# A hybrid backbone block (GDN, RWKV-7, mLSTM, mixture of experts): paired RWKV inverses, mLSTM on another chain, dense products in groups of six

## The chip, the cores and the metric

The kernel runs on one core of a Trainium2 chip. The metric is the device time of one execution in microseconds (us), the median of several runs. The profile is of one execution; its times count from the first instruction.

## The reference

Four layers. A layer takes 256 context tokens and 256 latent tokens of 1024 channels, modulates their RMS norm, and projects them by one matrix into the inputs of three mixers, each run in both directions, and 3 x 1024 gate columns. The three results are projected, gated, summed and projected again; a mixture of 16 experts follows. In the last layer the context tokens only feed states, and nothing else of them is computed.

```python
for l in range(DEPTH):
    gdn_x, rwkv_x, mlstm_x, gate_x = split_cols(modulate(rmsnorm(x)) @ w_in[l], col_groups)
    ...                                    # the same for the context tokens
    a_c, a_x = gdn_branch(...)             # 4 heads of 128: a unit lower triangular solve per chunk of 64, a scan
    b_c, b_x = rwkv_branch(...)            # 8 heads of 64: S_t = S_{t-1}(diag(w_t) + a_t b_t^T) + v_t k_t^T
    m_c, m_x = mlstm_branch(...)           # 4 heads, keys of 64, values of 128, stabilised by a running max
    x = x + mod_x[2] * (sum(sigmoid(gates[i]) * (branches[i] @ w_branch[i]) for i in range(3)) @ w_out[l])
    x = x + mod_x[5] * moe_ec(...)         # expert choice: each expert takes its best 32 tokens of 256
```

Latent scans start from the last state of the context scan of the same direction.

## The kernel before

All activations lie transposed, 128 channels by 512 tokens (256 of context, 256 latent). A layer's **scan stage** holds the input projection and the three mixers; behind it come the gated sum of the branches, the output projection and the experts.

**Dense products.** A block of 128 output columns is `w_in` (line 461): `load_w` brings the weights in two tiles of four 128x128 blocks, ScalarE rounds each to a high part (line 363), GpSimd subtracts to a low part (line 364), and `dense` (378) sums for each of eight k the products high x high, high x low and low x high, 24 products of 128x512 (256 wide in the last layer) into one PSUM bank. Two banks take such blocks: "dm" those that a mixer reads (31 a layer), "df" 36 fillers (gate columns, mLSTM's inputs), whose results go to DRAM.

**Order.** The program is not ordered by hand. Each instruction gets a priority from a planned time ("due", `at`, line 239), smaller first, and a list scheduler puts on each engine the ready instruction with the smallest one; the order is fixed when the program is built. `Stream.due` and `spend` move a mixer's due time on as its products are issued, by its pace. Before, RWKV has 240 due units per pair of heads (`D_R`), GDN 170 per head (`D_G`), mLSTM begins at 680 with pace 12 (`P_M`), and the fillers are spread over 1000. In `dense` three k (`CH`) share one due time, and anything with an earlier one may step in between two products. `go_on` (245) gives what follows the first call everywhere; only `ada`, the modulation's products, uses it.

**RWKV** runs four pairs of heads one after another on the PSUM banks "ai" and "ac". A pair has two units, context (`st` 0) and latent (`st` 1). A unit: `rwkv_prep` (decays, keys and so on, mostly VectorE, line 786), the masked products M (893), the transposes, `tri_inverse`, and four chunk steps (926). `rwkv_prep` of the next unit is issued inside `tri_inverse` of this one (`between`).

**`tri_inverse`** (393) inverts 16 systems of 64x64. They go to DRAM and come back as their 64 diagonal blocks of 16x16, a block per partition (so on 64 of 128 partitions); 14 column steps of two VectorE instructions invert these (413, 414); they go to DRAM and come back in place, and four rounds of 16 small products (437 to 440) give the inverse. GDN uses it once a head.

**GDN** runs four heads one after another on the banks "bi" (eight chunk steps a head, line 1120), and **mLSTM** follows GDN on the same banks, beside RWKV's last pairs. The first branch that is gated and projected, within mLSTM's stage, is GDN's; RWKV's and mLSTM's follow together behind the scans.

Of the kernel before, what the change touches and what calls it, by code (L numbers as in the profile page):

```python
# [12 lines left out]
U32 = mybir.dt.uint32  # L13
# [67 lines left out]
CH = 3  # L81
DT = BLK / 8 * 1.0
D_R, D_G = 240.0, 170.0
P_R, P_G, P_M = D_R * 2.6 / 240, D_G * 3.5 / 170, 12.0
# [68 lines left out]
def tile_backbone(ctx: ExitStack, tc: tile.TileContext, A, out, dbg=None, depth=DEPTH):  # L153
# [32 lines left out]
    for pi in ("ai", "bi"):  # L186
        systems[pi] = (dp.tile([2, 8, 4160], F32, tag="zi" + pi, bufs=1, name="zi" + pi),
                       dp.tile([2, 2, 8, 4160], F32, tag="zo" + pi, bufs=1, name="zo" + pi))
# [70 lines left out]
    with tc.tile_pool(name="zero", bufs=1) as p0:  # L259
        zero = p0.tile([128, 1040], F32, name="zero")  # L260
        gp.memset(zero, 0.0)
        for _, zo in systems.values():
            sy.dma_start(zo.rearrange("w p q x -> (w p q x)").rearrange("(a b) -> a b", a=128), zero)
# [30 lines left out]
    def ada(l, P, g, pool=None, bufs=2, t=None):  # L294
# [98 lines left out]
    def tri_inverse(z, src, sys, between=None):  # L393
        zi, zo = z.dram
        for p in range(2):
            sy.dma_start(zi[p, :, 0:4096].rearrange("q (r c) -> r q c", c=64), src(p))

        def blocks(t):
            return t.rearrange("p q x -> (p q x)").rearrange("(m x) -> m x", x=1040)[:, 0:1024].rearrange("m (r c) -> m r c", c=64)[:, :, 0:16]
        bt, sol = z.mt([2, 16, 16], "Y"), z.mt([2, 16, 16], "Z")  # L400
        bt, Xb = bt[0:64, 0], bt[0:64, 1]
        tr = "m r c -> m c r"
        sy.dma_start(bt, blocks(zi))
        md = [C[f"dir{d}"][0:64].bitcast(U32)[:, :, None].to_broadcast([64, 16, 16]) for d in range(2)]
# [10 lines left out]
        TU = z.mt([2, 8, 64], "TU")  # L415
        for w in range(2):
            xw, xo = (Xb, Xb.rearrange(tr)) if w == 0 else (Xb.rearrange(tr), Xb)
            se.copy(sol[0:64, w], xw)
            ve.copy_predicated(sol[0:64, w], md[1], xo)
            sy.dma_start(blocks(zo[w]), sol[0:64, w])  # L420
            for p in range(2):
                sy.dma_start(TU[64 * p:64 * p + 64, w], zo[w, p, :, 0:4096].rearrange("q (r c) -> r q c", c=64))
        T, U = TU[:, 0], TU[:, 1]
# [12 lines left out]
        Z, Y = z.mt([8, 64], "Z"), z.mt([8, 64], "Y")  # L436
        ve.tensor_tensor(Z, pz, C["off"][:, None, :].to_broadcast([128, 8, 64]), ALU.mult)
        last = U
        for _ in range(3):
            ve.tensor_tensor(Y, products(lambda p, hp, q: Z[hp, q, :], lambda p, hp, q: last[hp, q, :]), U, ALU.add)  # L440
            last = Y
        return T, U, Y
# [13 lines left out]
    def layer(l, P, last, ahead):  # L456
# [14 lines left out]
        gates = dp.tile([36, 128, 512], F32, tag="gates", name=nm("gates"))  # L471
# [9 lines left out]
        def first_branch():  # L481
# [3 lines left out]
            for b in range(4):  # L485
                t = w2k("lom")
                sy.dma_start(t[:, n], spill[0][:, b, n])
                split(ab[:, 0, b, n], ab[:, 1, b, n], t[:, n], gp)
            for db in range(8):
                at(AM0 + AMS * db)  # L490
                th = w2k("rawm")
                gated(0, db, (ab[:, 0], ab[:, 1]), th, "f")
                sy.dma_start(part[db][:, n], th[:, n])

        def second_branch():
            ab = big(F32R, (2, 4, 512))
            for b in range(4):
                t = wp.tile([128, 512], F32, tag=("him", "lom")[b % 2], bufs=2, name=nm("mg"))
                sy.dma_start(t[:, n], spill[1][:, b, n])
# [3 lines left out]
        def other_branches(z, rwkv_):  # L503
# [3 lines left out]
            for db in range(8):  # L507
                t1, th = t2(), t2() if db else wp.tile([128, 512], F32, tag="rawm", bufs=2, name=nm("mg"))
                gated(2, db, mlstm_, th, "f")
                gated(1, db, rwkv_, t1, "m")  # L510
# [9 lines left out]
        with scope("rwkv", "ai", "ac", 3) as zr:  # L520

            xT = X["sb"]
            r = rms_scale(zr, X["ss"], 0, "sgd")
            if l > 0:
                X["dram"] = dp.tile([128, 8, 512], F32, tag="xd", name=nm("xd"))
                sy.dma_start(X["dram"], xT)
            hh, hl = big(F32R), big(F32R)
            for k in range(8):
                t = zr.mt([512], "t2")
                ve.tensor_tensor(t, xT[:, k, :], r, ALU.mult)  # L530
                for s in range(2):
                    ts_ = t[:, s * 256:(s + 1) * 256]
                    ve.tensor_scalar(ts_, ts_, der[:, 0, k, s:s + 1], mod[:, k, s:s + 1], ALU.mult, ALU.add)
                split(hh[:, k, :], hl[:, k, :], t, gp)

            clock["base"] = tc.cur_priority + 100000


            todo = [(B_GATE + i, i) for i in range(24)] + [(B_MO + i, 24 + i) for i in range(4)]
            todo[FM:FM] = [(b + i, 28 + q + i) for b, q, m in ((B_MK, 0, 2), (B_MQ, 2, 2), (B_MV, 4, 4)) for i in range(m)]  # L540
            for t, (b, i) in zip(FILL, todo):
                c0 = 0 if i in (28, 29, 32, 33, 34, 35) else oc
                ps = w_in(b, t, c0, "f")
                th = common.mt([512], "gt", 1)
                if i < 28:
                    se.activation(th[:, c0:], ps[:, c0:], AF.Tanh, scale=0.5)  # L546
                else:
                    se.activation(th[:, c0:], ps[:, c0:], AF.Copy, scale=0.125 if i in (30, 31) else 1.0)
                sy.dma_start(gates[i][:, c0:], th[:, c0:])
            ahead()  # L550

            at(0)
            with scope("pre", "bi", "bi", 3) as z:
                G = small_gates(z, l, P, hh, hl)
            R = rwkv_begin(zr, l, P, w_in, oc)
            pair = [rwkv_inputs(zr, l, 0, P, R, w_in, oc)]
            S = {}

            def rwkv(b):
                rwkv_pair(zr, l, b, P, R, pair, S, spill[1], last, oc)  # L560
            with scope("gdn", "bi", "bi", 3) as zg:
                head = [gdn_inputs(zg, l, 0, P, w_in, oc), gdn_inputs(zg, l, 1, P, w_in, oc)]

                def gdn(h):
                    gdn_head(zg, l, h, P, head[h], G, spill[0], oc, D_G * h)
                pair.append(rwkv_inputs(zr, l, 1, P, R, w_in, oc))
                rwkv(0)
                gdn(0)
                head.append(gdn_inputs(zg, l, 2, P, w_in, oc))
                gdn(1)  # L570
                pair.append(rwkv_inputs(zr, l, 2, P, R, w_in, oc))
                rwkv(1)
                head.append(gdn_inputs(zg, l, 3, P, w_in, oc))
                gdn(2)
                pair.append(rwkv_inputs(zr, l, 3, P, R, w_in, oc))
                gdn(3)
            with scope("mlstm", "bi", "bi", 3) as zm:
                rwkv(2)
                rwkv(3)
                mlstm(zm, l, P, G, gates, oc, D_G * 4, first_branch)  # L580
                at(1500)
                rwkv_ = second_branch()


        with scope("moe", "ai", "bi") as z:
            W = Weights(z, l)
            rt = route_begin(z, l, P, last)
            mh, ml = other_branches(z, rwkv_)
# [1132 lines left out]
```

## Time and profile before

| | |
|---|---|
| median of 3 runs | 5148.35 us (5140.02 to 5159.23) |
| profiled execution | 5153.63 us, span 5151.7 us |
| busy: PE, VectorE, ScalarE, GpSimd | 4671.7, 3135.1, 1437.8, 1401.7 us |
| granted TensorE clock, mean | 0.95 |

PE is TensorE's products, PEld its weight loads, DVE VectorE, ACT ScalarE, POOL GpSimd, SPq the queue that issues all DMAs. The ends of products are modelled, so rows of PE overlap: the time that a product costs is read from start to start. Layer 1's scan stage runs from about 1420 to 2270 us, layer 3's from 4010 to 4790.

### The profile page before, as it was taken

The page shows a single profiled execution, that of the slowest core. Times are in us where ns is not written, and L with a number is a line of the kernel's source. Part 1 is how long each engine was busy: PE and PEld are TensorE (multiplying, and loading weights), DVE is VectorE, ACT ScalarE, POOL GpSimd, SP SyncE. Part 2 cuts the span into 40 slices and gives each one's busy share as a digit, 9 for nine tenths or more (in the row PEclk, how much of TensorE's full clock was granted, in tenths as well). Part 3 has the DMA queues.
Part 4 walks back from the last instruction along what each step waited for, and adds up shares of the span by engine and source line. Part 5 has one row for each costly group of instructions (what it writes and reads, how often), then busy time and mean ns, then how long its engine had stood idle before and what let it go on. Part 6 is the DMA issues. An engine that isn't in the chain of part 4 may idle for free. (4 is left out here: it accounts for less than half of the span.)

```text
span 5151.7 us, 85291 instructions
## 1 busy us (share of the span) xinstructions
PE 4671.7 (91%) x31882; PEld 2965.9 (58%) x31882; DVE 3135.1 (61%) x8787; ACT 1437.8 (28%) x2796; POOL 1401.7 (27%) x1847
## 2 busy tenths in 40 slices
PE   7999999999999989999998999999998898888698
PEld 4666666653466666665336666666633666666533
DVE  4777766633477876663347778666333688767322
ACT  3333232320233322222023323232201433222211
POOL 3333212320243332232014322223301433323400
PEclk8999999999999999999999999999999899987899
DMA  5334345679632233457972223345696222223598
GB/s 189 110 101 119 121 137 172 205 272 393 246 90 80 81 98 121 137 167 264 394 273 92 84 70 105 100 137 164 234 392 260 86 70 72 81 66 115 185 385 316
DMA packets 677006, 873.59 MB, mean 170 GB/s; under 512 B 336976, under 2 KB 359504, under 8 KB 663792
## 3 DMA queue, kind: packets, MB, share of 16 engines
q1 hardware_dynamic: 676592, 868.14, 50.0%
q8 instruction: 251, 4.11, 0.3%
q14 instruction: 163, 1.34, 0.1%
HBM read 788.47 MB, written 79.51 MB: 168 GB/s over the span
## 5 line engine op out<-in xcount | busy, mean ns | idle before, releaser
L364 POOL TENSOR_TENSOR wlo<-wraw,whi 128x512 fp32r<-128x512 f32 x696 | 938.3, 1353 | 2198.2 <-ACT whi L363 1649.3
L386 PE MATMUL df<-big,whi 128*128 128x512 f32 (+1 forms) x2944 | 1001.9, 408 | 87.6 <-ACT gt L546 19.7
L386 PE MATMUL dm<-big,whi 128*128 128x512 f32 (+1 forms) x2368 | 821.2, 415 | 44.6 <-ACT cv L693 31.7
L363 ACT CAST whi<-wraw 128x512 fp32r<-128x512 f32 x696 | 426.3, 617 | 1159.1 <-PE df L386 481.8
L386 PEld LDWEIGHTS df<-big,whi 128*128 128x128 f32 x2944 | 545.8, 200 | 253.9 <-issue 46.9
L386 PE MATMUL df<-big,wlo 128*128 128x512 f32 (+1 forms) x1536 | 612.0, 398 | 16.6 <-POOL wlo L364 16.6
L386 PEld LDWEIGHTS dm<-big,whi 128*128 128x128 f32 x2368 | 443.0, 199 | 174.6 <-issue 40.5
L386 PE MATMUL dm<-big,wlo 128*128 128x512 f32 (+1 forms) x1248 | 505.6, 405 | 18.3 <-POOL wlo L364 18.3
L386 PEld LDWEIGHTS df<-big,wlo 128*128 128x128 f32 x1536 | 306.3, 199 | 83.8 <-POOL wlo L364 20.9
L1607 PE MATMUL df<-mw,big 128*64 128x512 f32 x1024 | 301.3, 610 | 0.0
L386 PEld LDWEIGHTS dm<-big,wlo 128*128 128x128 f32 x1248 | 248.1, 199 | 81.2 <-POOL wlo L364 22.7
L1654 DVE SCALAR_TENSOR_TENSOR big<-bi,der,big 128x256 f32<-128x256 f32 x448 | 191.9, 478 | 118.4 <-PE bi L1651 117.9
L1607 PE MATMUL dm<-mw,big 128*64 128x512 f32 x1024 | 255.6, 594 | 2.3 <-DMA mw<-in_w_dram 2.3
L997 DVE SCALAR_TENSOR_TENSOR cv<-cv,par,cv 128x189 f32<-128x189 f32 (+3 forms) x472 | 231.3, 499 | 18.3 <-ACT cv L994 14.3
L1614 POOL MEMSET mada<- 128x512 f32 x32 | 16.8, 525 | 800.6 <-PE bi L1651 351.1
L414 DVE TENSOR_TENSOR Y<-Y,sv 64x14 f32<-64x14 f32 (+6 forms) x672 | 193.6, 290 | 5.6
L413 DVE TENSOR_TENSOR sv<-Y 64x14 f32<-64x14 f32 (+6 forms) x672 | 183.2, 275 | 5.4
L1607 PEld LDWEIGHTS dm<-mw,big 128*64 128x64 f32 x1024 | 80.7, 137 | 152.5 <-issue 137.8
L1645 DVE SCALAR_TENSOR_TENSOR mlof<-ac,aff,mhif 128x512 fp32r<-128x512 f32 x32 | 24.0, 750 | 212.4 <-ACT mhif L1644 212.4
L697 DVE SCALAR_TENSOR_TENSOR big<-cv,muc,big 128x252 f32<-128x252 f32 (+2 forms) x280 | 140.4, 515 | 21.0 <-ACT big L694 19.4
L1641 PE MATMUL ac<-mw,mrawf 128*64 128x512 f32 x512 | 139.6, 600 | 8.6 <-ACT mrawf L1635 8.5
L210 PE MATMUL ai<-AR,BK 64*128 64x128 f32 (+1 forms) x1024 | 133.4, 308 | 10.4 <-DVE M L893 6.1
(511 smaller groups left out, 7965.2 us busy)
## 6 DMA issues: line engine op xcount, KB each, us to landing
mw<-in_w_dram SPq DMA_DIRECT2D x768, 512.0 KB, 10.3
wraw<-in_w_in_dram SPq DMA_DIRECT2D x536, 256.0 KB, 2.7
adaw<-in_ada_w_dram SPq DMA_DIRECT2D x96, 1024.0 KB, 6.2
gates<-gt SPq DMA_DIRECT2D x114, 256.0 KB, 2.9
wraw<-in_w_branch_dram SPq DMA_DIRECT2D x96, 256.0 KB, 2.9
TU<-zoai SPq DMA_DIRECT2D x128, 128.0 KB, 3.1
wraw<-in_w_out_dram SPq DMA_DIRECT2D x64, 256.0 KB, 6.7
t<-gates SPq DMA_DIRECT2D x61, 256.0 KB, 4.1
```

Of the source, the lines that this page charges most:

```text
L210: mm(o, a, b, **kw)
L363: se.copy(dst_hi, src)
L364: eng.tensor_tensor(dst_lo, src, dst_hi.bitcast(F32), ALU.subtract)
L386: mm(ps[:, c0:c1], a[:, k % 4, :], bk[:, c0:c1], start=(n == 0), stop=(n == 3 * nk - 1))
L413: ve.tensor_tensor(tv, Xb[:, j + 1:, j:j + 1].to_broadcast(sh), Xb[:, j:j + 1, 0:j].to_broadcast(sh), ALU.mult)
L414: ve.tensor_tensor(Xb[:, j + 1:, 0:j], Xb[:, j + 1:, 0:j], tv, ALU.add)
L697: ve.scalar_tensor_tensor(dst, src, muc[:, 1 + q, rb:rb + 1], dst, ALU.mult, ALU.add)
L997: ve.scalar_tensor_tensor(dst, src, cw[:, cb, t:t + 1], dst, ALU.mult, ALU.add)
L1607: mm(ps[64 * q:64 * q + 64, :], xe[k // 4][:, k % 4, e0 + q, :], wt[q][:, k2 * 512:(k2 + 1) * 512], start=(k == 0), stop=(k == 7))
L1641: mm(py[hf][64 * q:64 * q + 64, :], hT[:, kk, 64 * q:64 * q + 64], wt[q][:, hf * 512:(hf + 1) * 512], start=(kk == 0), stop=(kk == 3))
L1645: ve.scalar_tensor_tensor(yl[hf], py[hf], aff, yh[hf].bitcast(F32), ALU.mult, ALU.subtract)
L1654: ve.scalar_tensor_tensor(xT[:, db, cs_], pcb[:, cs_], der[:, 3, db, s:s + 1], xT[:, db, cs_], ALU.mult, ALU.add)
```

## The change

1. `dense` takes two k at a time. The first of their six products (low x high of the second k) gets the due time; after each product `go_on` is called, so that the other five have first call.
2. RWKV's two units of a pair are prepared and loaded first (`rwkv_units`, `rwkv_unit`, `tri_load`), their 32 systems are inverted by one `tri_inverse` (128 blocks on 128 partitions, the four rounds of products for both), and then both units take their steps (`rwkv_steps`). The next pair's context unit is prepared after this pair's context steps, its latent unit after the end of this pair. M, the transposed keys and the values have two buffers; the key and receptance inputs have one instead of two.
3. The bonus term's product is formed at the end of the second preparation instead of at the pair's end.
4. GDN's output gate is stored to DRAM and read back at the end of the head.
5. mLSTM runs behind RWKV, on "ai" and "ac", while GDN's last head runs on "bi". Due times: 160 per RWKV pair, 210 per GDN head, mLSTM from 660 with pace 8. The first branch that is gated is RWKV's, and the order of the gate columns follows.
6. The modulation's weights have one buffer in `ahead` instead of two; the small gates' temporaries share one tile.

```diff
-CH = 3
+CH = 2
-D_R, D_G = 240.0, 170.0
-P_R, P_G, P_M = D_R * 2.6 / 240, D_G * 3.5 / 170, 12.0
+D_R, D_G, T_M = 160.0, 210.0, 660.0
+P_R, P_G, P_M = D_R * 2.6 / 240, D_G * 3.5 / 170, 8.0
...
     def dense(ps, w, rh, rl, nk, c0=0, c1=512, t=None):
         n = 0
-        for k in range(nk):
+        for k0 in range(0, nk, CH):
+            ks = range(k0, min(k0 + CH, nk))
+            terms = [(ks[-1], 2)] + [(k, q) for k in ks for q in range(3) if (k, q) != (ks[-1], 2)]
             if t is not None:
-                at(t + DT * CH * (k // CH))
-            hi, lo = w[k // 4]
-            for a, b in ((hi, rh), (hi, rl), (lo, rh)):
+                at(t + DT * k0)
+            for k, q in terms:
+                hi, lo = w[k // 4]
+                a, b = ((hi, rh), (hi, rl), (lo, rh))[q]
                 bk = b[k] if isinstance(b, list) else b[:, k]
                 mm(ps[:, c0:c1], a[:, k % 4, :], bk[:, c0:c1], start=(n == 0), stop=(n == 3 * nk - 1))
                 n += 1
+                if t is not None:
+                    go_on()
...
-    def tri_inverse(z, src, sys, between=None):
+    def tri_load(z, g, src):
+        for p in range(2):
+            sy.dma_start(z.dram[0][g, p, :, 0:4096].rearrange("q (r c) -> r q c", c=64), src(p))
+
+    def tri_inverse(z, ng, sys):
         zi, zo = z.dram
-        for p in range(2):
-            sy.dma_start(zi[p, :, 0:4096].rearrange("q (r c) -> r q c", c=64), src(p))
+        m = slice(0, 64 * ng)
...
-            tv = t[0:64, 0:(15 - j) * j].rearrange("m (r c) -> m r c", c=j)
-            sh = [64, 15 - j, j]
+            tv = t[m, 0:(15 - j) * j].rearrange("m (r c) -> m r c", c=j)
+            sh = [64 * ng, 15 - j, j]
...
-        if between:
-            between()
         at(z.t)
-        pz = products(lambda p, hp, q: sys(p, q), lambda p, hp, q: T[hp, q, :])
+        pz = [products(lambda p, hp, q: sys(g, p, q), lambda p, hp, q: T[g][hp, q, :]) for g in range(ng)]
...
+            with scope("mlstm", "ai", "ac", 3) as zm:
                 gdn(3)
-            with scope("mlstm", "bi", "bi", 3) as zm:
-                rwkv(2)
-                rwkv(3)
-                mlstm(zm, l, P, G, gates, oc, D_G * 4, first_branch)
+                mlstm(zm, l, P, G, gates, oc, T_M, first_branch)
...
-        rb, kb, vb = (ws[:, 3 * (b % 2) + q] for q in range(3))
+        kb, rb, vb, kds = (ws[:, q] for q in (0, 1, 2 + b % 2, 4 + b % 2))
...
+    def rwkv_units(z, l, b, P, R, pair, units, last, oc, sts=(0, 1)):
+        for st in sts:
+            noy = last and st == 0
+            z.due(D_R * (b - (0.3, 0.15)[st]), P_R * PS)
+            units[b, st] = rwkv_unit(z, b, st, pair[b]["vb"], noy, rwkv_prep(z, b, st, P, R, pair[b], noy, oc))
...
+        z.due(D_R * b, P_R * PS)
+        un = [units.pop((b, st)) for st in range(2)]
+        inv = tri_inverse(z, 2, lambda g, p, q: un[g]["M1"][64 * p:64 * p + 64, p, q // 4, q % 4, 0:64])
         S = None
         for st in range(2):
-            def between():
-                nb, ns = (b, 1) if st == 0 else (b + 1, 0)
-                if nb < 4:
-                    prs[nb, ns] = rwkv_prep(z, nb, ns, P, R, pair[nb], noy[ns])
-            z.due(D_R * (b + 0.5 * st) - OFF, P_R * PS)
-            S = rwkv_unit(z, b, st, vb, Y, S, noy[st], prs[b, st], between)
+            z.due(D_R * (b + 0.5 + 0.25 * st), P_R * PS)
+            S = rwkv_steps(z, st, un[st], inv[st], Y, S, last and st == 0)
+            if b < 3 and st == 0:
+                rwkv_units(z, l, b + 1, P, R, pair, units, last, oc, (0,))
...
-        zt = z.mt([512], "zt", 2)
+        zt = z.mt([512], "cv", CVB)
...
-        return KQ, v2, zt
+        sy.dma_start(gates[36 + h][:, n], zt[:, n])
+        return KQ, v2, gates[36 + h]
```

## Rows read from the trace of the kernel before

**Rows 1.** The page: span, busy time, one group of instructions, two kinds of DMA issue.
```profile
span 5151.7 us, 85291 instructions
...
PE 4671.7 (91%) x31882; PEld 2965.9 (58%) x31882; DVE 3135.1 (61%) x8787; ACT 1437.8 (28%) x2796; POOL 1401.7 (27%) x1847
...
L364 POOL TENSOR_TENSOR wlo<-wraw,whi 128x512 fp32r<-128x512 f32 x696 | 938.3, 1353 | 2198.2 <-ACT whi L363 1649.3
...
adaw<-in_ada_w_dram SPq DMA_DIRECT2D x96, 1024.0 KB, 6.2
...
t<-gates SPq DMA_DIRECT2D x61, 256.0 KB, 4.1
```

**Rows 2.** Stages: length, busy PE, PEld, DVE, ACT, POOL, granted clock, DMA share.
```profile
1420.00:2270.00 850.00, 789.20 (x6287) 545.59 (x6286) 624.99 (x1843) 272.12 (x545) 258.81 (x373) 0.96 0.35 105
...
4010.00:4790.00 780.00, 661.21 (x5773) 514.25 (x5773) 566.79 (x1694) 249.47 (x530) 271.41 (x395) 0.88 0.29 81
```

**Rows 3.** Stages, line 386 alone: length, busy PE (count), PEld, granted clock, DMA.
```profile
1420.00:2270.00 850.00, 480.73 (x1601) 288.34 (x1600) 0.96 0.35 105
...
2300.00:2325.00 25.00, 25.00 (x110) 20.15 (x109) 1.00 0.71 232
```

**Rows 4.** Timeline of PE, 1729 to 1734 us: start, us, instruction.
```profile
1729.03 0.50 PE L386 MATMUL df<-big,whi 128*128 128x512 f32 x1
1729.47 0.27 PE L210 MATMUL ai<-M,UV 128*64 128x64 f32 x1
...
1732.75 0.50 PE L386 MATMUL df<-big,whi 128*128 128x512 f32 x1
1733.18 0.45 PE L210 MATMUL ac<-R,Y 64*64 64x64 f32 x8
```

**Rows 5.** Timeline of PE: the first and last of 352 runs, their first rows.
```profile
1432.79 0.50 PE L386 MATMUL dm<-big,wlo 128*128 128x512 f32 x1
...
2264.69 0.70 PE L386 MATMUL df<-big,whi 128*128 128x512 f32 x2
```

**Rows 6.** Stage 1420 to 2270, lines 413 and 414 alone: length, busy DVE (count).
```profile
1420.00:2270.00 850.00, 44.52 (x168) 0.96 0.35 105
...
1420.00:2270.00 850.00, 48.81 (x168) 0.96 0.35 105
```

**Rows 7.** Waits of PE, 1420 to 2270: who for whom, us, times, longest.
```profile
PE ai L210 <- DVE Y L414: 2.2, 1, 2.2
```

**Rows 8.** Timelines of SP and DVE: ends of RWKV pairs (L781), GDN (L1206), mLSTM (L1424).
```profile
1667.11 1.43 SPq L781 DMA_DIRECT2D br<-t  x1
...
2232.72 0.42 SPq L781 DMA_DIRECT2D br<-t  x1
...
2040.58 0.33 SPq L1206 DMA_DIRECT2D br<-t  x1
...
2264.46 1.28 DVE L1424 TENSOR_TENSOR t<-bi,mKt 128x512 f32<-128x512 f32 x2
...
4261.16 0.33 SPq L781 DMA_DIRECT2D br<-t  x1
...
4785.69 0.33 SPq L781 DMA_DIRECT2D br<-t  x1
...
4638.24 0.32 SPq L1206 DMA_DIRECT2D br<-t  x1
...
4755.77 0.75 DVE L1424 TENSOR_TENSOR t<-bi,mKt 128x256 f32<-128x256 f32 x2
```

**Rows 9.** Timeline of DVE, one RWKV inverse and the preparation beside it.
```profile
1670.69 0.69 DVE L893 TENSOR_TENSOR M<-ai,cst 128x512 f32<-128x512 f32 x1
...
1676.00 0.69 DVE L828 TENSOR_TENSOR_SCAN t<-cst,t 128x256 f32<-128x256 f32 x1
...
1698.29 0.41 DVE L866 TENSOR_TENSOR BK<-t,t 64x256 f32<-64x256 f32 x1
...
1725.47 0.69 DVE L440 TENSOR_TENSOR Y<-ai,TU 128x512 f32<-128x512 f32 x1
```

More of the change, by code (lines that the diff above doesn't have):

```diff
@@ L185, in tile_backbone @@
     systems = {}
-    for pi in ("ai", "bi"):
-        systems[pi] = (dp.tile([2, 8, 4160], F32, tag="zi" + pi, bufs=1, name="zi" + pi),
-                       dp.tile([2, 2, 8, 4160], F32, tag="zo" + pi, bufs=1, name="zo" + pi))
+    for pi, ng in (("ai", 2), ("bi", 1)):
+        systems[pi] = (dp.tile([ng, 2, 8, 4160], F32, tag="zi" + pi, bufs=1, name="zi" + pi),
+                       dp.tile([2, ng, 2, 8, 4160], F32, tag="zo" + pi, bufs=1, name="zo" + pi))
     class Stream:
@@ L262, in tile_backbone @@
         for _, zo in systems.values():
-            sy.dma_start(zo.rearrange("w p q x -> (w p q x)").rearrange("(a b) -> a b", a=128), zero)
+            for w in range(2):
+                zw = zo[w].rearrange("g p q x -> (g p q x)").rearrange("(a b) -> a b", a=128)
+                sy.dma_start(zw, zero[:, 0:zw.shape[1]])
     fg = cp.tile([128, 8], F32, name="fg")
@@ L470, in layer @@
         spill = [dp.tile([128, 4, 512], F32, tag=f"br{i}", name=nm("br")) for i in range(2)]
-        gates = dp.tile([36, 128, 512], F32, tag="gates", name=nm("gates"))
+        gates = dp.tile([40, 128, 512], F32, tag="gates", name=nm("gates"))
         part = dp.tile([8, 128, 512], F32, tag="part", name=nm("part"))
@@ L518, in other_branches @@
             return mh, ml
[L520 to L562, printed above, removed]
@@ new lines, in layer, with rwkv @@
+        with scope("gdn", "bi", "bi", 3) as zg:
+            with scope("rwkv", "ai", "ac", 3) as zr:
+                xT = X["sb"]
+                r = rms_scale(zr, X["ss"], 0, "sgd")
+                if l > 0:
+                    X["dram"] = dp.tile([128, 8, 512], F32, tag="xd", name=nm("xd"))
+                    sy.dma_start(X["dram"], xT)
+                hh, hl = big(F32R), big(F32R)
+                for k in range(8):
+                    t = zr.mt([512], "t2")
+                    ve.tensor_tensor(t, xT[:, k, :], r, ALU.mult)
+                    for s in range(2):
+                        ts_ = t[:, s * 256:(s + 1) * 256]
+                        ve.tensor_scalar(ts_, ts_, der[:, 0, k, s:s + 1], mod[:, k, s:s + 1], ALU.mult, ALU.add)
+                    split(hh[:, k, :], hl[:, k, :], t, gp)
+                clock["base"] = tc.cur_priority + 100000
+                todo = [(B_GATE + i, i) for i in (*range(8, 16), *range(8), *range(16, 24))] + [(B_MO + i, 24 + i) for i in range(4)]
+                todo[FM:FM] = [(b + i, 28 + q + i) for b, q, m in ((B_MK, 0, 2), (B_MQ, 2, 2), (B_MV, 4, 4)) for i in range(m)]
+                for t, (b, i) in zip(FILL, todo):
+                    c0 = 0 if i in (28, 29, 32, 33, 34, 35) else oc
+                    ps = w_in(b, t, c0, "f")
+                    th = common.mt([512], "gt", 1)
+                    if i < 28:
+                        se.activation(th[:, c0:], ps[:, c0:], AF.Tanh, scale=0.5)
+                    else:
+                        se.activation(th[:, c0:], ps[:, c0:], AF.Copy, scale=0.125 if i in (30, 31) else 1.0)
+                    sy.dma_start(gates[i][:, c0:], th[:, c0:])
+                ahead()
+                at(0)
+                G = small_gates(zg, l, P, hh, hl)
+                R = rwkv_begin(zr, l, P, w_in, oc)
+                pair = [rwkv_inputs(zr, l, 0, P, R, w_in, oc)]
+                S = {}
+                def rwkv(b):
+                    rwkv_pair(zr, l, b, P, R, pair, S, spill[1], last, oc)
+                head = [gdn_inputs(zg, l, 0, P, w_in, oc, gates), gdn_inputs(zg, l, 1, P, w_in, oc, gates)]
@@ L564, in gdn @@
                 def gdn(h):
                     gdn_head(zg, l, h, P, head[h], G, spill[0], oc, D_G * h)
+                rwkv_units(zr, l, 0, P, R, pair, S, last, oc)
                 pair.append(rwkv_inputs(zr, l, 1, P, R, w_in, oc))
@@ L610, in small_gates, with sc @@
     def small_gates(z, l, P, hh, hl):
-        wsr = z.mt([8, 32], "wsr")
+        buf, o = z.mt([1024], "TU"), [0]
+        def sc(*shape):
+            o[0] += math.prod(shape)
+            v = buf[:, o[0] - math.prod(shape):o[0]]
+            return v.rearrange("p (a b) -> p a b", a=shape[0]) if len(shape) == 2 else v
+        wsr = sc(8, 32)
         sy.dma_start(wsr, A["w_sm"][l])
@@ L783, in rwkv_pair, with rwkv_prep @@
             sy.dma_start(dbg["b"][:, b, :], av)
-    def rwkv_prep(z, b, st, P, R, pr, noy):
+        if b < 3:
+            rwkv_units(z, l, b + 1, P, R, pair, units, last, oc, (1,))
+    def rwkv_prep(z, b, st, P, R, pr, noy, oc):
         rb, kb, ups = pr["rb"], pr["kb"], pr["ups"]
@@ L894, in rwkv_unit @@
                                  C[f"m1_{d}"][:, None, 0:w_].to_broadcast([128, 4, w_]), ALU.mult)
[L896 to L897 removed]
+        BKt = z.mt([8, 128], "BKt", 2)
+        UV = z.mt([2, 4, 2, 64], "UV", 2)
         for d in range(2):
@@ L985, in rwkv_unit, with gdn_inputs @@
         return X
-    def gdn_inputs(z, l, h, P, w_in, oc):
+    def gdn_inputs(z, l, h, P, w_in, oc, gates):
         cw = P["conv"].rearrange("p (b t) -> p b t", b=12)
```

140 lines of the change are left out of this document (75 added, 65 removed).

## The prediction

> **What bounds the kernel now.** I read the page first: PE is busy for 4671.7 of 5151.7 us, no other engine for two thirds of that [rows 1]. So either PE's own work shrinks, or little happens. Next the busy time by stage. A layer's scan stage (projection, RWKV, GDN, mLSTM) takes 850 us in layer 1, of which PE idles 850 - 789.2 = 61 us; in layer 3, which computes only half of the dense columns, it is 780 - 661.2 = 119 us of idle time [rows 2]. What PE spends there is read from line 386 alone. In a stretch with nothing but dense products one costs 25.00 / 110 = 0.227 us; in the scan of layer 1 the same line is busy 480.73 us for 1601 products, 0.300 each [rows 3]. The PE timeline shows why: small products of the scans stand between one or two dense ones. A single dense product there holds PE 0.43 us from its start to the next small product's (1729.03 to 1729.47, 1732.75 to 1733.18) [rows 4]. I counted the runs of consecutive line-386 products in that timeline: 352 runs with 1558 products begin in layer 1's scan, and 288 of them are shorter than six and hold 757 products together (first and last run in [rows 5]); layers 0 and 2 have 360 and 351 runs, layer 3 has 257, of which 176 with 477 products are short. So PE is the bound, and a good part of its time is broken runs.
>
> **Holding six products together.** The number of products stays. The 288 short runs of layer 1 become at fewest 757 / 6 = 126 sixes: 162 runs fewer. At most every six stands alone: 1558 / 6 = 260 runs, 92 fewer. I take the middle, 126. Price of a run: (480.73 - 1601 x 0.227) / 352 = 0.33 us at most [rows 3], since part of that surplus is the granted clock of 0.96 [rows 2]; a single product's way out alone costs 0.43 - 0.227 = 0.20 us [rows 4], which I take for the least, because the small products on both sides now meet and are often of another shape. I take 0.27, between the two. That is 126 x 0.27 = 34 us a layer, 102 us for layers 0 to 2, with bounds of 92 x 0.20 = 18 and 162 x 0.33 = 53 us a layer. In layer 3, 0 to 96 runs go; half of it, 48 x 0.27, is 13 us.
>
> The Trainium skill speaks against the full price: TensorEngine Tiling (Array Packing), section Tiling Modes, says that changing the tiling mode, and not merely the tile, drains TensorE. The trace agrees as far as 0.43 against 0.227 us goes [rows 3, 4]. By that rule a run that goes between small products of two modes leaves one drain where there were two, so that it saves nearer 0.20 than 0.33 us: 25 instead of 34 us a layer.
>
> What holding costs: a small product that becomes ready inside a six waits up to 6 x 0.227 = 1.36 us, 0.68 on average, where one product makes it wait 0.11. That lengthens the chains of RWKV, GDN and mLSTM, and costs time only where no dense product is left to fill the gap. Bounds: 0, and, if half of the some 280 bursts of small products that RWKV's PSUM banks take in that stretch (counted in the same timeline) hit a six and nothing fills, 140 x 0.57 = 80 us a layer. I take 10 us for layers 0 to 2, near the lower end, because the gaps are filled today but for 61 of 850 us [rows 2]: 30 us.
>
> The first product of each group now reads the low part of the weights, which POOL makes 1.35 us after ACT's high part [rows 1]. POOL is busy 259 of 850 us [rows 2] and the weights are double buffered, so I cost it at 0; with that cover gone it is 1.35 us for each of 67 blocks, 90 us a layer.
>
> **Paired inverses.** Eight RWKV systems a layer become four of twice the partitions; the four of GDN stay. Lines 413 and 414 run 168 times each in layer 1's scan for 44.5 and 48.8 us, that is for 12 solves [rows 6]; a third goes, 31 us of VectorE a layer, and four DMA round trips with it. PE's count of products stays. PE waits on this loop for 2.2 us in that scan [rows 7], since dense products fill, so I count 0 in layers 0 to 2. If instead each us of DVE were on the path, it would be 31 us a layer.
>
> **RWKV's chain.** A pair takes (2232.72 - 1667.11) / 3 = 188.5 us in layer 1 and (4785.69 - 4261.16) / 3 = 175 us in layer 3 [rows 8]. One inverse, from the last mask product M to the end of the third Y, takes 1726.2 - 1670.7 = 55 us [rows 9]. One of the two in a pair goes. Against it the next pair's second preparation, which runs beside an inverse now (DVE works on it from 1676.0 to 1698.7, the middle rows of that group), must wait until the steps give back their buffers: some 20 us. So 35 us less a pair, four pairs 140 us: RWKV would end at 2233 - 140 = 2093 in layer 1 and at 4646 in layer 3.
>
> **mLSTM behind RWKV.** It runs from GDN's end to its own last product now: 2040.6 to 2265.7, 225 us, and in layer 3, with half of the tokens, 4638.2 to 4756.5, 118 us [rows 8]. Behind RWKV it would end between 2093 + 118 = 2211 and 2093 + 225 = 2318 in layer 1; today's scan chains end at 2266. At its new pace (8 instead of 12) it has first call where it had last call, so I take the lower half and no cost. In layer 3 it would end at 4646 + 118 = 4764, where RWKV ends now at 4786: 22 us less, of which I keep 15 for the longer waits of the held products there.
>
> **Edits at nothing.** GDN's output gate goes through DRAM: one store and one load of 256 KB a head, two more issues of 0.33 us each on SP's queue (as the issues of that size in [rows 8]); the load waits for nothing but a buffer and so starts well before its use. Uncovered, the 4.1 us that such loads take to land on the page's list [rows 1] would stand once in each head of GDN, 16 us a layer on a chain that has room. The adaLN weights lose their second buffer: 1 MB lands in 6.2 us [rows 1], and eight such loads are planned over 180 of the due units of which a layer has 1000 in about 900 us, one every 20 us. RWKV's key and receptance lines lose theirs, too: the projection of the next pair waits for this pair's second preparation, and with it PSUM's "dm" bank; "df" fills meanwhile. The order of the gates and the bonus product moved into the preparation change no count.
>
> **The sum**, for the profiled execution, whose span is 5151.7 us and whose own time is 5153.6, 5.3 us above the median of three, 5148.35: - 102 - 13 (runs) + 30 (waits) - 15 (layer 3's chain) = -100. Against the median that is **5048 us**. With the bounds of the runs alone: 3 x 18 to 3 x 53 and 0 to 25, so 5120 to 4965.
>
> **Rivals.**
> 1. The chain becomes the end (slower). RWKV and mLSTM are now one chain with every stage waiting for sixes. It decides as soon as mLSTM takes longer than 2266 - 2093 = 173 us in layer 1; then the dense products are used up and PE idles. At 200 us it adds 27 us a layer, at 225 us 52, and what the runs save goes into idle time: 5148 + 3 x 27 = 5230, up to 5300. For it: 225 us today, more work on one chain, mean wait 0.68 us. Against it: mLSTM's pace is set by due times today, and it does half the work in 118 us. 22%.
> 2. The switch only moves (no change). Small products of different shapes meet where a dense run was, runs fall by the 92 of the lower bound at 0.15, and the 30 us of waits eat the rest: 3 x 92 x 0.15 = 41 less, 30 more, about 5140. For it: the scans alternate between several shapes every 0.4 us [rows 4]. 13%.
> 3. Chain and idle time gain as well. The 31 us of VectorE and the shorter chain also take away half of the idle time and of what the clock lost (0.96 and, in layer 3, 0.88 granted [rows 2]): 30 us more in each of layers 0 to 2 and 40 in layer 3, 5148 - 100 - 130 = 4920. 10%.
>
> My forecast has 55%, with its own range from 4965 to 5120. A measurement of this kernel tells about 0.5% (26 us) from no change. Faster takes nearly all of the forecast and rival 3; of rival 1 the mild end, where mLSTM takes little over 173 us, ends as no change. Faster 0.63, same 0.16, slower 0.21. The range for 8 in 10 reaches from rival 3's time to that of rival 1: 4925 to 5230.
>
> **What would show it.** Right: no run of line 386 in the projection under six; 190 to 260 runs in layer 1's scan; that line's busy time there down from 481 to about 445 us at the same count; 112 instead of 168 calls of lines 413 and 414; RWKV's pairs 150 us apart; PE idle in the scan of layers 0 to 2 within 50 to 75 us. Wrong: the line's busy time falls but PE's idle time in the last 150 us of the scan rises by as much, with mLSTM's rows the last to end (rival 1); or runs fall and the busy time of the small products (line 210) rises as much (rival 2); or PE begins to wait for POOL's low part at the head of the blocks.

## The result and the profile after

The changed kernel takes **5071.44 us** (median of 4 runs, 5064.11 to 5077.79) where the kernel before takes 5145.93 beside it: a ratio of 0.9848, 95% interval 0.983 to 0.9866; 0.0152 of 5148 is 78 us (the two medians differ by 74). The time is 23 us above the forecast of 5048 and inside its own range. The profiled execution has a span of 5070.9 us against 5151.7.

The page of the kernel after; these lines answer to [rows 1]:

```profile
span 5070.9 us, 84827 instructions
...
PE 4530.9 (89%) x31882; PEld 2946.4 (58%) x31882; DVE 3067.7 (60%) x8291; ACT 1417.9 (28%) x2748; POOL 1432.1 (28%) x1831
...
L367 POOL TENSOR_TENSOR wlo<-wraw,whi 128x512 fp32r<-128x512 f32 x696 | 943.5, 1360 | 1969.4 <-ACT whi L366 1806.5
...
adaw<-in_ada_w_dram SPq DMA_DIRECT2D x96, 1024.0 KB, 5.9
...
t<-gates SPq DMA_DIRECT2D x73, 256.0 KB, 3.5
```

PE executes the same 31882 products in 141 us less, but the span falls by only 81: PE's idle time (span less busy) rose from 480 to 540 us. Where this happens is seen in the scan stages, with the columns of [rows 2]; the first row is layer 1, the second layer 3, the third the last 125 us of layer 1's scan:

```profile
1400.00:2245.00 845.00, 763.80 (x6333) 549.15 (x6331) 606.29 (x1722) 269.30 (x535) 268.99 (x371) 0.94 0.38 114
3960.00:4712.00 752.00, 631.87 (x5794) 503.56 (x5794) 546.55 (x1583) 244.83 (x518) 274.51 (x389) 0.87 0.31 86
2125.00:2250.00 125.00, 100.63 (x533) 73.05 (x530) 96.31 (x297) 28.43 (x55) 24.48 (x26) 0.77 0.42 134
```

In layer 1 PE is idle 81 instead of the 61 us of [rows 2]. The same last 125 us of the kernel before were fuller and ran at a mean granted clock of 0.99 instead of 0.77 (a mean of the two levels, 2.4 and 1.2 GHz):

```profile
2145.00:2270.00 125.00, 114.36 (x798) 82.65 (x797) 85.64 (x232) 36.10 (x63) 40.94 (x37) 0.99 0.41 131
```

The dense line alone (now line 393) in layer 1's stage, answering to [rows 3]:

```profile
1400.00:2245.00 845.00, 444.31 (x1607) 298.43 (x1605) 0.94 0.38 114
```

480.73 became 444.31 us at the same count. The small products' helper (line 210, now 211) did not take it over; before and after, each kernel with its own line:

```profile
1420.00:2270.00 850.00, 322.20 (x4346) 231.54 (x4346) 0.96 0.35 105
```

```profile
1400.00:2245.00 845.00, 302.31 (x4346) 223.06 (x4346) 0.94 0.38 114
```

The two lines' busy times overlap where a run meets a small product, so what PE gained is read from its whole busy time. From 50 us behind the layer's begin to the end of the chains, before and after:

```profile
1415.00:2266.00 851.00, 791.50 (x6297) 547.56 (x6296) 621.27 (x1839) 273.24 (x547) 258.83 (x372) 0.96 0.34 105
```

```profile
1397.00:2239.00 842.00, 762.29 (x6316) 548.50 (x6315) 601.85 (x1716) 268.49 (x534) 266.94 (x368) 0.94 0.38 114
```

PE lost 29 us of busy time, not 36 + 20, and its idle time rose from 59 to 80. The same stretches of layers 0 and 2 gave 34 and 32 us, and idle times of 73 and 82. The timeline of PE shows what [rows 4] showed, with a whole six between two small products:

```profile
1699.78 0.44 PE L211 MATMUL bi<-Vt,Y 64*64 64x128 f32 x4
1700.15 0.50 PE L393 MATMUL dm<-big,wlo 128*128 128x512 f32 x1
1700.48 0.62 PE L393 MATMUL dm<-big,whi 128*128 128x512 f32 x2
1700.95 0.40 PE L393 MATMUL dm<-big,wlo 128*128 128x512 f32 x1
1701.18 0.62 PE L393 MATMUL dm<-big,whi 128*128 128x512 f32 x2
1701.73 0.49 PE L211 MATMUL bi<-v2g,Kt 64*128 64x128 f32 x4
```

Start to start the six holds PE for 1701.73 - 1700.15 = 1.58 us, 0.22 more than 6 x 0.227. Counted in that timeline, layer 1's scan has 200 runs (352 before), layers 0, 2 and 3 have about 205, 200 and 160. The runs that are shorter than six all lie in the first branch's products, from 778 us into the layer on, which are not held.

The solve's two instructions (now lines 428 and 429), the waits of PE in the stage, and the ends of the chains answer to [rows 6], [rows 7] and [rows 8]; the waits behind the solve's lines are 10.2 us, where they were 2.2:

```profile
1400.00:2245.00 845.00, 28.10 (x112) 0.94 0.38 114
...
1400.00:2245.00 845.00, 37.00 (x112) 0.94 0.38 114
```

```profile
PE ai L211 <- DVE BK L895: 8.8, 6, 2.3
PE ai L215 <- DVE mH L1448: 7.8, 1, 7.8
PE dm L393 <- DVE sv L428: 5.2, 1, 5.2
PE ai L211 <- DVE Y L429: 5.0, 1, 5.0
```

```profile
1346.88 0.63 ACT L348 ACTIVATE t<-big 128x512 f32<-128x512 f32 x1 [0.15 <-DVE big L1694]
...
1659.76 0.33 SPq L809 DMA_DIRECT2D br<-t  x1
...
2117.75 0.42 SPq L809 DMA_DIRECT2D br<-t  x1
...
2187.66 0.32 SPq L1246 DMA_DIRECT2D br<-t  x1
...
2238.29 0.68 DVE L1464 TENSOR_TENSOR t<-ai,mKt 128x512 f32<-128x512 f32 x1
```

The first of these rows, the last square of the layer's norm, is taken as the layer's begin. Before, the layer began at

```profile
1364.92 0.63 ACT L345 ACTIVATE t<-big 128x512 f32<-128x512 f32 x1 [0.15 <-DVE big L1654]
```

so that, counted from the layer's begin, RWKV's first pair ended at 302 us and ends at 313, its last at 868 and 771, GDN at 676 and 841, and mLSTM, the last to end, at 900 and 891 (the first number is before, the second after). From begin to begin the four layers take 1326, 1303, 1300 and 1168 us before and 1306, 1287, 1287 and 1134 after: 20, 16, 13 and 34 us less.

### The profile page after: what moved, and what is told of

It is laid out like the page before. It is cut to its first block, busy times and chain, and to the rows that moved or that the text cites. A ratio compares the mean times of both kernels' runs of the same rounds, so it can differ in the third digit from the quotient of the medians.

```text
span 5070.9 us, 84827 instructions
## 1 busy us (share of the span) xinstructions
PE 4530.9 (89%) x31882; PEld 2946.4 (58%) x31882; DVE 3067.7 (60%) x8291; ACT 1417.9 (28%) x2748; POOL 1432.1 (28%) x1831
## 5 line engine op out<-in xcount | busy, mean ns | idle before, releaser
L393 PE MATMUL df<-big,whi 128*128 128x512 f32 (+1 forms) x2944 | 897.0, 385 | 1.7 <-POOL big L367 1.7
L393 PE MATMUL dm<-big,whi 128*128 128x512 f32 (+1 forms) x2368 | 732.1, 388 | 0.0
L393 PE MATMUL df<-big,wlo 128*128 128x512 f32 (+1 forms) x1536 | 648.3, 422 | 54.8 <-ACT gt L565 13.5
L393 PEld LDWEIGHTS df<-big,whi 128*128 128x128 f32 x2944 | 564.2, 200 | 97.0 <-issue 6.5
L393 PE MATMUL dm<-big,wlo 128*128 128x512 f32 (+1 forms) x1248 | 521.2, 418 | 46.9 <-POOL wlo L367 13.4
L1034 DVE SCALAR_TENSOR_TENSOR cv<-cv,par,cv 128x189 f32<-128x189 f32 (+3 forms) x472 | 243.2, 527 | 38.3 <-ACT cv L1031 33.8
L722 DVE SCALAR_TENSOR_TENSOR big<-cv,muc,big 128x255 f32<-128x255 f32 (+2 forms) x280 | 158.1, 587 | 27.1 <-ACT big L719 24.8
L211 PE MATMUL ai<-AR,BK 64*128 64x128 f32 (+1 forms) x1024 | 104.6, 311 | 62.0 <-DVE BK L895 32.2
L211 PEld LDWEIGHTS ai<-AR,BK 64*128 64x128 f32 x1024 | 85.9, 207 | 96.0 <-issue 33.2
L308 PE MATMUL ad<-adaw,cs 128*32 128x512 f32 x768 | 116.5, 659 | 26.2 <-DMA adaw<-in_ada_w_dram 21.4
## 6 DMA issues: line engine op xcount, KB each, us to landing
mw<-in_w_dram SPq DMA_DIRECT2D x768, 512.0 KB, 10.2
```

Of the source, the lines that this page charges most:

```text
L211: mm(o, a, b, **kw)
L308: mm(ps[32 * j:32 * j + 32, :], cs[:, k, :], wt[:, j, :], start=(k == 0), stop=(k == 7), tile_position=(0, 32 * j))
L722: ve.scalar_tensor_tensor(dst, src, muc[:, 1 + q, rb:rb + 1], dst, ALU.mult, ALU.add)
L1034: ve.scalar_tensor_tensor(dst, src, cw[:, cb, t:t + 1], dst, ALU.mult, ALU.add)
```

## The experiments

Each ran five rounds beside the kernel before. Ratios are to that, with 95% intervals. The columns on the right are read in the profiled execution, in layer 1's scan: runs of the dense line; its busy time and PE's idle time, from 50 us behind the layer's begin to the chains' end (for the kernel before, in the window of [rows 2]); and when the last of the chains ended, from the layer's begin.

| kernel | us | ratio | runs | line, us | idle, us | chains' end |
|---|---|---|---|---|---|---|
| before | 5145.93 | 1 | 352 | 481 | 61 | 900 |
| after | 5071.44 | 0.9848 [0.983, 0.9866] | 200 | 443 | 80 | 891 |
| e1 change without holding | 5149.94 | 0.9995 [0.9981, 1.0009] | 322 | 471 | 65 | 901 |
| e2 before with holding | 5135.95 | 0.9972 [0.9961, 0.9983] | 200 | 451 | 81 | 911 |
| e3 inverses one by one | 5102.16 | 0.9913 [0.9898, 0.9928] | 199 | 447 | 81 | 901 |
| e4 fillers due later | 5069.3 | 0.9849 [0.9834, 0.9864] | 193 | 441 | 71 | 893 |
| e5 after, short solves | 4964.02 | 0.9638 [0.9625, 0.9652] | 203 | 440 | 59 | 868 |
| e6 e2, short solves | 4952.26 | 0.9617 [0.9604, 0.963] | 209 | 435 | 52 | 859 |
| e7 before, short solves | 5026.2 | 0.9757 [0.9737, 0.9778] | 333 | 480 | 43 | 883 |
| e8 GDN due at 190 | 5051.98 | 0.9814 [0.9799, 0.9829] | 189 | 435 | 81 | 884 |
| e9 solves aside | 4997.97 | 0.9703 [0.968, 0.9725] | 203 | 438 | 64 | 873 |
| e10 RWKV 140, GDN 190 | 5067.76 | 0.9835 [0.9815, 0.9855] | 201 | 440 | 76 | 897 |
| e11 twelves | 5212.67 | 1.0117 [1.0099, 1.0136] | 122 | 413 | 113 | 933 |
| e12 threes | 5092.32 | 0.9877 [0.9855, 0.9898] | 266 | 465 | 66 | 893 |

**The two halves alone.** e1 takes the holding out of the changed kernel, e2 puts the change's `dense` into the kernel before and nothing else.

```diff
                 n += 1
-                if t is not None:
-                    go_on()
```

> The changed kernel without the calls of go_on in dense: the groups of six have one due time again, but small products may step in between them. Theory A (broken runs of dense products are what PE's time goes into, and the hold is the gain): runs of dense products in layer 1's scan rise from 199 to over 320, line 393's busy time there from 444 to about 480 us, PE's idle time in the scan falls by some 20 us a layer, time about 5125 (5105 to 5150). Rival B (the shorter RWKV chain and the removed VectorE work are the gain, the hold costs as much as it gives): 5075 or less.

> The kernel before with nothing but the new dense (groups of six, low part first, held together). Theory A: runs fall from 352 to about 200 in layer 1's scan and line 386's busy time by 36 us, but RWKV's unpaired chain gets longer by its waits and eats a part: 5100 (5070 to 5130). Rival B: the unpaired chains, each stage waiting for sixes, become the end, idle time at the end of the scan rises by 50 us a layer: 5150 to 5250, no faster than before.

The new structure alone gains nothing, holding alone 13 us, both together 78. So holding is needed, as theory A has it, but neither theory foresaw that it needs the structure. The zero of e1 is itself a sum of two. The begins of layer 3 and of the final norm behind it, in the kernel before, in e1 and in the changed kernel:

```profile
3967.55 0.63 ACT L345 ACTIVATE t<-big 128x512 f32<-128x512 f32 x1 [0.15 <-DVE big L1654]
5135.42 0.81 ACT L345 ACTIVATE t<-big 128x256 f32<-128x256 f32 x2 [1.43 <-DVE big L1654]
```

```profile
3983.79 0.63 ACT L348 ACTIVATE t<-big 128x512 f32<-128x512 f32 x1 [0.15 <-DVE big L1692]
5132.00 0.81 ACT L348 ACTIVATE t<-big 128x256 f32<-128x256 f32 x2 [1.43 <-DVE big L1692]
```

```profile
3920.56 0.63 ACT L348 ACTIVATE t<-big 128x512 f32<-128x512 f32 x1 [0.15 <-DVE big L1694]
5054.33 0.81 ACT L348 ACTIVATE t<-big 128x256 f32<-128x256 f32 x2 [1.43 <-DVE big L1694]
```

The structure alone costs 16 us in layers 0 to 2 and gives 20 in layer 3. Holding added to it gives 63 us up to layer 3's begin and 14 in layer 3. (These are single executions: layer 3 of e4, whose median is that of the changed kernel, took 14 us longer there.) In layer 1 of e1, GDN's last head ends at 792 us into the layer instead of 676, and mLSTM at 901, as late as before.

In e2 the runs fell as far as in the changed kernel and the dense line's busy time by 30 us. What it gave back is in the window of its layer 1 scan (columns of [rows 2]) and in its chains' ends:

```profile
1398.00:2260.00 862.00, 780.59 (x6326) 563.82 (x6324) 639.47 (x1846) 271.73 (x549) 265.29 (x375) 0.95 0.36 105
```

```profile
1347.93 0.63 ACT L345 ACTIVATE t<-big 128x512 f32<-128x512 f32 x1 [0.15 <-DVE big L1660]
...
2258.81 0.33 SPq L787 DMA_DIRECT2D br<-t  x1
```

```profile
2238.67 0.68 DVE L1430 TENSOR_TENSOR t<-bi,mKt 128x512 f32<-128x512 f32 x1
```

RWKV's last pair ends at 2258.81, 911 us into the layer (868 before), 20 us behind mLSTM, and PE is idle 81 instead of 61 us.

**Are the chains what ends a scan?** e5, e6 and e7 cut each solve of `tri_inverse` to its last column step: 13 of 14 steps are left out, all else is issued as before.

```diff
-        for j in range(1, 15):
+        for j in range(14, 15):
```

> The changed kernel with only the last of the 14 column steps of each solve (the inverses are then wrong; everything else is issued as before). PE's work is the same; the chains are shorter by some 7.5 us per solve (busy 65 us for 8 solves in layer 1's scan, 13/14 of it): 30 us a layer for RWKV, 30 for GDN, and VectorE has 60 us a layer less to do. Theory C (the chains end the scan of the changed kernel: the tail of layer 1 runs at 0.77 granted clock with the fillers used up 114 us before the end): the scan becomes 15 to 30 us shorter a layer, 4960 to 5015 us. Theory D (PE's own work is the bound, the idle time is scattered): under 10 us a layer, 5035 to 5071.

> The old structure with groups of six held together, and the solves cut to their last column step (inverses wrong). Theory C (holding gained only 13 us there because RWKV's chain, whose last pair ended 915 us into layer 1, behind everything else, became the end): eight solves fewer in that chain, some 58 us a layer, so 5136 falls by 30 to 50 us a layer, to 4940 to 5015. Theory D: it stays above 5090.

> The kernel before with the solves cut to their last column step (inverses wrong): the control. If PE's broken runs are its bound, both theories expect little here: 5110 to 5150. If it falls as far as the other two, the chains were the bound before as well.

With short solves holding alone is worth 5026.2 - 4952.26 = 74 us where it was worth 13, and the structure is worth nothing more on top (4964.02 against 4952.26; 12 us the other way). That is theory C, and it is the core of the case: holding gains little where the chains leave no room, and whatever makes room, the structure or short solves, lets it gain. (Short solves also take work off VectorE, which the next run tries to set apart.) The control went against its expectation: the kernel before gained 124 us too. Layer 1's windows of e7 and e6:

```profile
1388.00:2222.00 834.00, 790.90 (x6310) 548.03 (x6310) 572.25 (x1528) 273.13 (x547) 259.84 (x373) 0.97 0.37 107
```

```profile
1368.00:2178.00 810.00, 757.81 (x6288) 545.24 (x6288) 581.97 (x1530) 270.98 (x545) 259.40 (x372) 0.97 0.38 110
```

In e7 PE's work in the stage is what it was in [rows 2] (790.90 against 789.20) and its idle time fell from 61 to 43 us. So the solves set part of the time already before, at a PE that was 93% busy.

**Latency, or VectorE's work?** In e9, 13 of the 14 steps read a constant, and nobody reads their result.

```diff
-        for j in range(1, 15):
+        for j in range(14, 15):
...
+        at(z.t + 20)
+        for j in range(1, 14):
...
+            ve.tensor_tensor(tv, J, J, ALU.mult)
+            ve.tensor_tensor(tv, J, tv, ALU.add)
```

> The changed kernel with 13 of the 14 column steps of each solve done on a constant with a result that nobody reads, due 20 units later (the inverses are wrong, as where the steps were left out): VectorE executes the same number of instructions of the same shapes, but the chain from the mask product to the inverse no longer holds them. Theory C (the latency of the chains is what the steps cost): as with the steps left out, 4964, up to 4990. Theory E (VectorE's work is what they cost, since others queue behind it): 5040 to 5075.

Between the two: of the 107 us that short solves give in the changed kernel (e5), 73 are gained with VectorE's work still done, and 34 are not. The idle work is due 20 units later here and so steps aside more easily than the solve's own; 34 may be less than it costs in its place. The two windows, e9 first, then e5, show the same PE work; VectorE is busy 41 us more and PE idle 5 us more in e9:

```profile
1364.00:2187.00 823.00, 758.86 (x6316) 546.00 (x6315) 605.98 (x1715) 267.24 (x533) 265.17 (x368) 0.95 0.39 116
```

```profile
1362.00:2181.00 819.00, 760.28 (x6317) 546.46 (x6316) 565.33 (x1508) 266.84 (x532) 264.51 (x368) 0.95 0.40 117
```

**What the pairing is worth.** e3 keeps all of the change, but inverts a pair's two units by two calls one after the other (the edits that give these calls tiles of their own are left out here).

```diff
...
-        inv = tri_inverse(z, 2, lambda g, p, q: un[g]["M1"][64 * p:64 * p + 64, p, q // 4, q % 4, 0:64])
+        inv = [tri_inverse(z, 1, lambda _, p, q, g=g: un[g]["M1"][64 * p:64 * p + 64, p, q // 4, q % 4, 0:64], g, 2)[0] for g in range(2)]
```

> The changed kernel, in which a pair's two units are prepared together as there, but inverted by two calls one after the other, each on 64 partitions as before; the rest is the same. Theory A1 (RWKV's chain with mLSTM behind it is the end of the scan in the changed kernel, so each us on it counts): VectorE gets 31 us a layer back, each pair takes some 15 to 20 us longer, mLSTM begins 60 to 80 us later, and the scan ends 40 to 80 us later in each layer: 5071 + 4 x 60 = 5310 (5230 to 5390). Rival B1 (PE's throughput is the end, the inverse lies beside it): under 5100.

31 us, between the theories. e3's first and last pair in layer 1, whose begin is at 1339.42, and the begins of its layer 3 and of its final norm:

```profile
1650.20 0.33 SPq L811 DMA_DIRECT2D br<-t  x1
...
2111.07 0.38 SPq L811 DMA_DIRECT2D br<-t  x1
```

```profile
3931.09 0.63 ACT L348 ACTIVATE t<-big 128x512 f32<-128x512 f32 x1 [0.15 <-DVE big L1696]
5087.16 0.81 ACT L348 ACTIVATE t<-big 128x256 f32<-128x256 f32 x2 [1.43 <-DVE big L1696]
```

The pairs are (2111.07 - 1650.20) / 3 = 153.6 us apart, and the last ends 772 us into the layer: both as in the changed kernel. So the paired inverse is not what shortened RWKV's chain; what else the structure does for it (both units prepared ahead of the inverses, more buffers, other due times) did. Of the 31 us the profiled execution shows 22 in layer 3 and 10 before it, with VectorE busy 22 us more in layer 1's scan (624 against 602) and GDN and mLSTM ending 10 us later there. Holding alone being 13, some 34 us are left for the rest of the structure, mLSTM's place and the due times together; these were not run apart.

**How long a group.** `CH` = 1 and 4, three and twelve products held:

```diff
-CH = 2
+CH = 4
```

> The changed kernel with one k, three products, held together (CH = 1). Twelves lost 141 us although their runs fell from 200 to 122 and the line's busy time by 30 us in layer 1. Theory G (the price of holding grows faster than the length, so six is already beyond the best): runs about 250 to 270, the chains end 10 to 20 us earlier, 5035 to 5065. Theory H (up to six the runs weigh more): the line's busy time rises by 12 to 18 us a layer in layers 0 to 2, 5085 to 5120.

> The changed kernel with four k, twelve products, held together (CH = 4). By the prediction's terms: at least 1600 / 12 = 133 runs in layer 1's scan where there are 200, at most 67 fewer, at 0.27 us 18 us a layer; the mean wait of a small product goes from 0.68 to 1.36 us, another 10 us a layer or more: 5045 to 5075. Theory C: the chains lose more than the runs gain, 5080 to 5140.

None, three, six, twelve held: 5150, 5092, 5071 and 5213 us. Threes came out by theory H, though in the profiled execution layers 1 and 2 took no longer than with sixes (1287 and 1283 us against 1287 each). Twelves came out as theory C has it, and 73 us above its range. Layer 1's scan with twelves, and its last 126 us:

```profile
1442.00:2326.00 884.00, 771.25 (x6328) 570.27 (x6327) 604.43 (x1714) 267.94 (x533) 270.05 (x369) 0.91 0.37 109
...
2200.00:2326.00 126.00, 98.64 (x506) 70.77 (x506) 91.68 (x296) 25.00 (x51) 19.62 (x20) 0.72 0.36 120
```

The dense line's busy time fell by another 30 us, 0.38 per run that went. But each link of the chains waits longer: GDN's last head ends at 882 instead of 841, RWKV at 804 instead of 771, the fillers are used up 703 us into the layer, 230 before the chains' end, and PE idles 113 us in the scan.

**The tail.** In the changed kernel the last filler ends 778 us into layer 1, 113 before the chains. e4 makes the fillers due 1.15 times later, so that they last; e8 and e10 change the due times of the chains.

```diff
+FILL = [t * 1.15 for t in FILL]
...
-D_R, D_G, T_M = 160.0, 210.0, 660.0
+D_R, D_G, T_M = 160.0, 190.0, 660.0
```

(e8; e10 has 140, 190 and 600.)

> The changed kernel with the fillers' due times stretched by 1.15 (0 to 1111 instead of 0 to 966). Theory A2 (in the last 120 us of a scan the fillers are used up, PE idles and its clock falls, and fillers kept for then cost less): the last filler ends 60 us or more later in layer 1, clock in the last 125 us of the scan over 0.9 instead of 0.77, 10 to 20 us a layer: 5015 (4990 to 5045). Rival B2 (the scheduler puts a filler wherever PE has nothing else, whatever its due time): fillers end where they did, 5071 within 15.

> The changed kernel with 190 instead of 210 due units per GDN head. GDN's last head ended 64 us behind RWKV's last pair in layer 1 (841 against 777). Theory C: GDN ends earlier, its last head lies less alone, tail clock above 0.77, 5 to 10 us a layer less, 5030 to 5055. Theory D: 5071 within 12.

> The changed kernel with 140 due units per RWKV pair (160), 190 per GDN head (210) and mLSTM from 600 (660). With 190 alone it took 5052, and in layer 1 mLSTM's last product came 112 us behind RWKV's end at 772. Theory C: RWKV called earlier ends earlier, and mLSTM with it: another 5 to 10 us a layer, 5010 to 5035. Theory F (a pair is held by its own waits, not by its call): RWKV's end does not move, 5045 to 5065.

Fillers due later change nothing (the last one ends at 784 us): the scheduler takes whatever is ready into a gap, due or not. GDN called earlier (e8) beats both kernels, 5052 us: GDN ends at 815, and layer 1's last 125 us run at 0.90:

```profile
2104.00:2229.00 125.00, 101.00 (x576) 72.26 (x577) 98.49 (x293) 35.30 (x68) 33.37 (x35) 0.90 0.47 151
```

Calling RWKV earlier too (e10) did not move its end in layer 1 (771), as theory F has it, and the time lies just above that theory's range. GDN's end went back to 840, and what e8 gained in layers 1 and 2 was gone; only layer 0 became shorter. How due times of this size act on single layers (layer 0 took 1276 us in e10, 1305 in e8; layer 1 1291 and 1277) I cannot derive; e8's 19 us are measured, not explained beyond its tail.

## Why the prediction came out as it did

**Right.** The direction and most of the size: 78 us of 100. *Runs:* 152 fewer in layer 1 (I took 92 to 162, and 126); the dense line's busy time fell by 36 us there, 34 were predicted. PE as a whole gave 29 to 34 us in layers 0 to 2. It is the change's engine, as e1 shows: holding added to the structure gave 63 us in layers 0 to 2, where -34 + 10 a layer makes 72, and 14 in layer 3, where 13 were predicted. *Solves:* 112 calls each, and a solve is hardly longer for twice the systems: 8.3 us on 128 partitions against 8.0 on 64 in the same scan. *Layer 3:* its chains end 35 us earlier (818 to 783 from the layer's begin) and the layer is 34 us shorter; 28 were predicted, 15 of them from the chain, where e1 shows 20, though with the runs at the top of their bound (97 fewer, not 48). *mLSTM:* 2238 - 2118 = 121 us behind RWKV, in the lower half as taken and under the 173 us at which rival 1 decides. *Covers:* POOL's low part is made in 1.36 us as before, and PE waits for it 1.9 us in layer 1's scan, as before.

**Right by luck.** *The pair:* (2117.75 - 1659.76) / 3 = 152.7 us, 153.5 predicted, because "one of the two in a pair goes". But e3 keeps both inverses of a pair and has 153.6, so that step is not what made the pairs shorter. *The price of a run:* in layer 1 PE gave 29 us for 152 runs, 0.19 us each and not 0.27, at a lower granted clock (0.94 against 0.96). From e7 to e6, both at 0.97, it gave 33 us for 124 runs, 0.27 us each, of which 5 us are 22 products fewer in the window at 0.227 each. So more runs went than I took and each gave less, and the two errors cancel. *The range:* by the prediction's own terms its bounds are 5148 - 39 = 5109 and 5148 - 169 = 4979, not 5120 and 4965; the measured time lies in both.

The Trainium skill's rule on tiling modes (TensorEngine Tiling (Array Packing), section Tiling Modes: a change of mode drains TensorE) argued for 25 us a layer instead of 34, because small products of two modes would meet. Counted in PE's timeline, changes of the products' tile shape in layer 1's scan fell from 771 to 553, those between two small products rose only from 166 to 212, and the small products' line became 20 us cheaper. With fewer changes in all, the rule speaks for the change here. What a run gave PE as a whole, 0.19 to 0.27 us, covers both prices and does not decide between them, and no run shows the price of a single change of mode. Rival 2 falls: the small products' line did not rise.

**Mis-sized: what stood at nothing, and the waits.** Layer 3 begins 47 us earlier than before, where -34 + 10 a layer makes 72. Of the 25 us that are missing, e1 puts 16 on the structure and 9 on holding. The step that failed is the zero for the structure in layers 0 to 2: "no cost" for mLSTM's new place and due times, 0 for the paired inverses. I reasoned "because the gaps are filled today", as though the fillers made a chain's length free so long as mLSTM did not end late. e7 shows that this was not so even before.

In layer 1 the chains' end moved from 900 to only 891. RWKV's last pair ends 97 us earlier (I had 140), since the first pair, for which I also took 35 us off, ends 11 us later than before (its two preparations now stand ahead of the inverse; that this is why was not run apart). GDN's last head ends at 841 instead of 676: at 792 already with the structure alone, the rest with sixes between its steps. Of what PE saved in work, 21 us came back as idle time, 14 of them in the last 125 us, where no filler is left. With 80 and 82 us in layers 1 and 2, PE's idle time also left the 50 to 75 us that I had named as a sign of being right. That is rival 1's mechanism in a mild form, on GDN's last head and mLSTM together, though not at the point that I gave for it.

So the terms as measured: holding 74 us where short solves leave room, 77 in the profiled executions on the new structure (I had -115 + 30 = -85 for runs and waits), 13 on the old one; the pairing 31 us, most of it in layer 3. Even the changed kernel's chains leave not quite enough room: with short solves it falls by another 107 (e5), 73 of them without less work on VectorE (e9). Rival 3 said that the shorter chain would also give back idle time and clock. Idle time did not fall, and not because of holding alone: in e1, without it, it is 65 us against 61, and the chains end at 901.

What stays open: 7 of layer 1's 16 us came behind the scan (402.6 to 395.4 us from mLSTM's last product to the next layer), which no step foresaw and no run took apart; in e2, where RWKV ends behind mLSTM, the same stretch took 415. Which part of the structure makes RWKV's pairs shorter, and which makes layers 0 to 2 longer without holding, was not run apart either.

## What to carry to other kernels

Where a list scheduler mixes a long run of independent products with dependent chains, holding the products in groups buys engine time and pays with chain latency, so price it against the slack of the chains, not against the idle time shown: take most of a link's latency out (by leaving steps out) and see whether the gain grows. Keep the work itself in a second run, as e9 does, or the two are mixed. Tune the group's length: here three, six and twelve gave 58, 79 and -63 us against none held. And two edits that measure nothing and 0.3% apart can be worth 1.5% together, when one spends the slack that the other makes. Last, a number that comes out as predicted does not show its reason: the pairs' 153 us did, and e3 has them without the edit that was to make them.

## What the runs showed of the hardware

Short VectorE instructions on twice the partitions cost little more: in layer 1's scan of the changed kernel the solve's two took 262 and 310 ns on 64 partitions (GDN's solves) and 240 and 351 on 128 (RWKV's), 572 and 591 ns together. The mean granted clock of layer 1's scan went from 0.97 with 43 us of idle time in e7 to 0.94 with 80 after and 0.91 with 113 in e11, but not by the amount of idle time alone: e8 had 0.96 with 81 us, and its last 125 us ran at 0.90, where those of the changed kernel ran at 0.77.
